# Emitting the small products of a recurrent head's scores block by block, sorted by shape

## The chip, the cores and the metric

The kernel runs on one core of a Trainium2 chip. The metric is the device time of one execution in microseconds (us); three executions of the kernel before took 1355.1, 1355.35 and 1356.38 us, median 1355.35. A profile of one execution tells when each instruction of each engine ran. TensorE multiplies matrices (PE in the profile; its weight loads are PEld), VectorE (DVE), ScalarE (ACT) and GpSimd (POOL) do the elementwise work, and SyncE (SP) issues most transfers.

## The reference

Two trunk layers over 512 latent tokens and 256 context tokens of width 1024. The first layer's mixer has eight neighbourhood attention heads and four bidirectional gated recurrent heads (HGRN2); the change lies in these four heads. Cut to that:

```python
def hgrn2_scan(q, k, v, log_f, s0):
    # S_t = diag(f_t) S_{t-1} + k_t v_t^T, o_t = S_t^T q_t, in chunks of 32 tokens
    def step(state, inp):
        qc, kc, vc, gc = inp
        bcum = jnp.cumsum(gc, axis=2)
        btot = bcum[:, :, -1:]
        qe = qc * jnp.exp(bcum)
        ke = kc * jnp.exp(-bcum)
        att = jnp.where(causal_in_chunk, jnp.einsum('bhtk,bhsk->bhts', qe, ke), 0.0)
        o = jnp.einsum('bhtk,bhkv->bhtv', qe, state) + jnp.einsum('bhts,bhsv->bhtv', att, vc)
        kd = kc * jnp.exp(btot - bcum)
        new_state = jnp.exp(btot)[:, :, 0, :, None] * state + jnp.einsum('bhsk,bhsv->bhkv', kd, vc)
        return new_state, o
...
    for d in range(2):          # forwards and backwards, each with its own gates
        ol, _ = hgrn2_scan(tr(qh), tr(k), tr(v), tr(lf), s_ctx)
        o_lat = o_lat + tr(ol)
    y = _hg_readout(o_lat, g, norm_w)
```

## The kernel before

All dense products run on TensorE in three parts (high by high, high by low, low by high part of float32; helper `mm3`, lines 246 to 248), in slices of 128 contraction rows against 512 latent or 256 context tokens. A class `Weave` puts background work between such slices: a task is a generator that yields how many slices its next step should stay behind. The order in which the code emits instructions is each engine's order, apart from what the framework's scheduler moves on the other engines; TensorE works through its list from the front, and an instruction that waits holds all behind it.

A recurrent head has two directions. `direction` makes, for each, decayed queries and keys by scans on VectorE: `qn`, `kn` within blocks of 32 tokens, `ke` for the keys of the same block, `qb` and `kb` for pairs of blocks within 128 tokens by half (GpSimd, line 608), `qi` and the states `st` at the starts of the four blocks of 128. When both directions are done, `head` runs with steps in between: `scores(0)`, `scores(1)`, `outputs(0)`, `outputs(1)`, then a root mean square.

`scores(half)` fills one bank of the accumulator memory (`pa`, 128 x 512) with four squares of 128 x 128: two blocks of 128 tokens (`nn`) by two directions (`d`). Within a square the 128-token score is put together from three kinds of products: a whole one from `ke` and `qn` (line 661), whose diagonal blocks of 32 are right; over it a 64 x 64 one from `kb` and `qb` (line 663); and over that two 32 x 32 ones from `kn` and `qn` (line 667), each with a position of its own among the array's column groups (`tile_position=(0, r0)`, r0 = 0 and 64 forwards, 32 and 96 backwards). The 64 x 64 one goes to output rows 0 to 63 forwards, 64 to 127 backwards. These are float32, which TensorE runs as two passes, so the profile counts two for each. VectorE then copies the allowed half of each square to `att` (line 671, a predicated copy) and adds the two directions to `as` (line 675); `outputs(half)` uses `as` as a weight (line 684) beside `st` and `qi` (line 682), and ScalarE starts the root mean square from the result.

Head 0's two calls have wide products between them. In heads 1, 2 and 3 the two calls come directly behind each other. The next direction's `pkc` (transposes, line 584) follows them in heads 1 and 2. Other names that the rows show: `pf`, `pfc` are the projections of gates for latent and context tokens, `pu` the state updates (line 639), `pm` an early product over four column groups (line 339), `pno` the attention's product with the values, which alternates between two 64-column tiles (line 846), `whi` and `wlo` the two parts of a weight.

Of the kernel before, what the change touches and what calls it, by code (L numbers as in the profile page):

```python
# [18 lines left out]
P = 128  # L19
# [19 lines left out]
class Weights:  # L39
    """Streams weight chunks and splits each sub-block exactly into two float32r parts."""  # L40

# [23 lines left out]
    def conv(self):  # L65
        """Split the next sub-block."""
        if self.nsub >= len(self.subs):
# [25 lines left out]
    def get(self, ahead=1):  # L93
        """The next sub-block, with some more split ahead of their use."""
        self.ahead(1 + ahead)
        r = self.ready[self.ncall]
        self.ncall += 1
        return r


class Weave:
    """Background work emitted between slices of a dense stream; a task yields the number of
    slices that its next step should stay behind."""

# [29 lines left out]
def backbone(ctx: ExitStack, tc: tile.TileContext, a, out, dump=None):  # L134
# [12 lines left out]

    # ---------------------------------------------------------------- pools
    cp = ctx.enter_context(tc.tile_pool(name="cp", bufs=1))
# [4 lines left out]

    # ---------------------------------------------------------------- weight plan
    ktiled = lambda w: w.rearrange("(k p) c -> p k c", p=P)
# [15 lines left out]
    plan = []  # L172
# [27 lines left out]

    # ---------------------------------------------------------------- constants
    cst = cp.tile([P, 769], F32, name="cst")
# [16 lines left out]

    # ================================================================ start  # L220
    m1 = ExitStack()
# [12 lines left out]
    def gate(h, src):  # L234
        """Output gate of a recurrent head with its norm weight."""
        t = zp.tile([P, T], F32, tag=f"z{4 + h}", name=f"gg{h}")
        S.activation(t[:], src, AF.Sigmoid)
        V.scalar_tensor_tensor(t[:], src, pv[:, 48 + h : 49 + h], t[:], ALU.mult, ALU.mult)
        gg[h] = t
# [10 lines left out]
    def rms(srcs, n, nm, pool, aux):  # L250
        """Reciprocal root mean square over the features."""
        acc = pool.tile([P, n], F32, tag="sqa" + nm, name="sqa" + nm, bufs=1)
# [34 lines left out]
    with ExitStack() as st:  # L287
# [36 lines left out]

        # (1 + bias) * norm weight
        wb = sp.tile([P, KT], F32, name="wb")
        V.scalar_tensor_tensor(wb[:], abT[:, 8:16], 1.0, pv[:, 16:24], ALU.add, ALU.mult)

        # adaptive shift and scale of latents and context, one feature tile at a time;
        # row blocks of the weights go to the four column groups of the array  # L330
        def normed(k):
# [29 lines left out]

        # sum of squares: odd tiles straight on the tensor engine
        acc = sp.tile([P, T], F32, name="sqax")
# [38 lines left out]

        # lower bounds of the forget gates
        lb = sp.tile([P, 24], F32, name="lb")
# [24 lines left out]
    for m in range(4):  # L429
        dbg(f"qh{m}", qf[m])  # L430
    # ---------------------------------------------------------------- remaining adaptive vectors
    class Ada:
        """Products of the remaining adaptive weights with silu(c), a row block and half a vector at a time."""

# [53 lines left out]

    # ================================================================ mixer of layer 0
    wv = Weave()  # L490
# [28 lines left out]

    # values of the recurrent heads, token-major  # L520
    wv.add(ada_units(11, 6))
# [21 lines left out]

    # ---------------------------------------------------------------- recurrent heads
    v32 = lambda t: t.rearrange("p (n t) -> p n t", t=32)
    dirs = {}

    def direction(h, d, s, sc):
# [6 lines left out]

        # weights of the context keys for the state after the context
        fc = hp.tile([P, TC + 2], F32, tag="fc", name=f"fc{nm}", bufs=1)
# [10 lines left out]

        # products of the gates within blocks of 32, up to a token and from it on
        fg = hp.tile([P, T + 2], F32, tag="fg", name=f"fg{nm}", bufs=1)  # L570
# [19 lines left out]
        V.tensor_copy(tb[:, 1:17], qn_[:, tot::32])  # L590
        # carries between blocks: [0] from the start, [1] to the end, of 128 and of 64
        cv = hp.tile([P, 4, 16], F32, tag="cv", name=f"cv{nm}", bufs=2)
# [32 lines left out]
        yield 2  # L625
        # states at the start of each block of 128
        pk = aux_t(f"pkt{nm}")
# [20 lines left out]
    def head(h):  # L648
# [5 lines left out]
        def scores(half):  # L654
            pt = aux_t(f"pa{h}{half}")
            for nn in range(2):
                n = 2 * half + nn
                for d, (qn_, kn_, ke, qi, qb, kb, st) in enumerate(hd):
                    c0 = (nn * 2 + d) * P
                    ts = slice(n * P, (n + 1) * P)  # L660
                    TE.matmul(pt[:, c0 : c0 + P], ke[:, ts], qn_[:, ts], start=True, stop=True, skip_group_check=True)
                    r0, t0 = (0, 64) if d == 0 else (64, 0)
                    TE.matmul(pt[r0 : r0 + 64, c0 + t0 : c0 + t0 + 64], kb[:, n], qb[:, n], start=True, stop=True,
                              skip_group_check=True)
                    for z in (0, 64):
                        r0, t0 = (z, z + 32) if d == 0 else (z + 32, z)
                        TE.matmul(pt[r0 : r0 + 32, c0 + t0 : c0 + t0 + 32], kn_[:, n * P + r0 : n * P + r0 + 32],
                                  qn_[:, n * P + t0 : n * P + t0 + 32], start=True, stop=True, skip_group_check=True,
                                  tile_position=(0, r0))
            a_ = att[half]  # L670
            V.copy_predicated(a_[:].rearrange("p (n c) -> p n c", n=2), dims(hgm[:], [0, 2], [1, 256]),
                              pt[:].rearrange("p (n c) -> p n c", n=2))
            am[half] = hp.tile([P, 2, P], F32, tag="as", name=f"as{h}{half}", bufs=2)
            a4 = a_[:].rearrange("p (n d c) -> p n d c", n=2, d=2)
            V.tensor_tensor(am[half][:], a4[:, :, 0], a4[:, :, 1], ALU.add)
# [16 lines left out]
        outputs(1)  # L692
        # root mean square over the head's value dimension
        sq = hp.tile([P, T], F32, tag="fg", name=f"osq{h}", bufs=1)
# [23 lines left out]

    # keys and values of the attention heads, feature-major, columns grouped by 16
    def permuted(dst, src):  # L720
# [33 lines left out]

    # ---------------------------------------------------------------- neighbourhood attention
    nas = ExitStack()
# [6 lines left out]
    def attention():  # L763
        """16 columns of queries against 32 of keys and the context at a time, two heads abreast."""
        pair, todo = {}, []
# [17 lines left out]
        def begin(p_):  # L783
            # float32r parts, stacked along the contraction: keys as (hi, lo), queries as (hi, hi) and (lo, lo)
            KS = np_.tile([P, 2, T + TC], F32R, tag="KS", name=f"KS{p_}", bufs=2)
# [122 lines left out]

    # first columns of the output projection, the last attention heads as they come
    w_first = [ws.get() for _ in range(2)]  # L910
# [11 lines left out]

    # ================================================================ the dense rest
    xp = ctx.enter_context(tc.tile_pool(name="xp", bufs=1, side="right", reuse_waits="tile"))
# [13 lines left out]
    class Norm:  # L938
        """Sum of squares over features, then the modulated norm in float32r parts."""

# [10 lines left out]
        def back(self, o, m, c, gate):  # L951
            """x += gate * o"""
            pin(V.scalar_tensor_tensor(xT[m][:, c], o[:, c], gate[:, m : m + 1], xT[m][:, c], ALU.mult, ALU.add))
# [17 lines left out]
        def outs(self, c):  # L971
            """Yields after each step of the eight feature tiles."""
            u = {}
# [12 lines left out]
    def project_back(nm, src, groups, gate, norm, start=0):  # L986
        """x += gate * (src @ w), feature-major, with the next norm; returns what the next
        phase has to emit while its first half runs."""
        A, B = HALF
# [56 lines left out]
    def pair(nm, src):  # L1046
        """Two output tiles of a 256-column chunk."""
        w = [ws.get(), ws.get()]
        o = [acc_t(f"pp{nm}{i}") for i in range(2)]
        for i in range(2):  # L1050
            mms(o[i], w[i], src, 0, 0, KT, slice(0, T), True, True)
        return o

    def quad(nm, src, rest):
        """Four output tiles, half of the tokens at a time while the norm is still on its way."""
        w = [ws.get(0) for _ in range(4)]
# [77 lines left out]

    # short convolution mixer
    mix = []
# [35 lines left out]

    # last projection, token-major
    fw = yp.tile([P, D], F32, tag="y4", name="fw")
# [107 lines left out]
```

## Time and profile before

| | kernel before |
|---|---|
| time, median of 3 runs (lowest, highest) | 1355.35 us (1355.1, 1356.38) |
| span of the profiled execution | 1353.2 us |
| median of the runs less that span | 2.15 us |
| TensorE matmuls busy | 1330.6 us, 98% |
| VectorE busy | 819.5 us, 61% |
| ScalarE busy | 527.8 us, 39% |
| GpSimd busy | 84.4 us, 6% |
| first call of `scores` starts, last ends | 131.00, 235.13 us |

The span runs from the first to the last instruction; the profiled execution has no other time of its own, so its whole time is taken as the span plus what the median of the runs lies above it. Busy time of matmuls is modelled from their starts, so a stretch in which TensorE is busy throughout can still hold time in which the array does no work; it shows in the distance from start to start.

### The profile page before, as it was taken

To read this page: it belongs to the slowest core of one execution; us is meant where nothing else is said; L and a number is where in the kernel's file an instruction comes from. 1 tells how busy PE (TensorE), PEld (TensorE's weight loads), DVE (VectorE), ACT (ScalarE), POOL (GpSimd) and SP (SyncE) were. 2 spreads that over 40 slices of the span, in tenths; PEclk is the share of its full clock that TensorE was granted. 3 is DMA by queue.
4 is the path that set the end of the run, shared out by engine and by line. 5 is a ranking of instruction groups with operands and counts; after the bars stand their busy time and mean duration, and the time that the engine had idled before them with its cause. 6 is when DMAs were issued, how large, how long until landed. Compare 5 with 4: busy or idle time off the path is not lost. (4 is left out here: it accounts for less than half of the span.)

```text
span 1353.2 us, 19127 instructions
## 1 busy us (share of the span) xinstructions
PE 1330.6 (98%) x7736; PEld 1134.4 (84%) x7736; DVE 819.5 (61%) x1354; ACT 527.8 (39%) x815; POOL 84.4 (6%) x87
## 2 busy tenths in 40 slices
PE   7999999999999999999999999999999999999997
PEld 4797888888879888888888898888998888889997
DVE  4668788687777645555566675557766544442333
ACT  4533444555555433333322253223443333333223
POOL 2204322321000000000000000000000000000000
PEclk9999999999999999999999999999999999999999
DMA  9942112466454233333366633444423222332231
GB/s 295 267 127 65 32 32 78 117 159 178 146 168 143 90 117 128 124 118 117 109 192 196 211 126 125 149 143 152 147 86 124 94 94 95 102 101 84 86 110 63
DMA packets 170824, 172.21 MB, mean 127 GB/s; under 512 B 14320, under 2 KB 144752, under 8 KB 170736
## 3 DMA queue, kind: packets, MB, share of 16 engines
q1 hardware_dynamic: 168736, 166.15, 39.3%
q10 hardware_dynamic: 2000, 4.85, 1.4%
q8 instruction: 60, 0.98, 0.3%
q14 instruction: 28, 0.23, 0.1%
HBM read 165.21 MB, written 2.10 MB: 124 GB/s over the span
## 5 line engine op out<-in xcount | busy, mean ns | idle before, releaser
L84 ACT CAST whi<-wraw 128x1024 fp32r<-128x1024 f32 (+1 forms) x202 | 207.8, 1031 | 471.1 <-PE ppv L247 93.5
L85 DVE TENSOR_TENSOR wlo<-wraw,whi 128x1024 fp32r<-128x1024 f32 (+1 forms) x202 | 242.7, 1203 | 218.9 <-ACT whi L84 217.6
L247 PE MATMUL ppa<-hf,whi 128*128 128x512 f32 (+1 forms) x448 | 161.6, 361 | 0.0
L246 PE MATMUL ppa<-hf,whi 128*128 128x512 f32 (+1 forms) x448 | 161.2, 360 | 0.0
L248 PE MATMUL ppa<-hf,wlo 128*128 128x512 f32 (+1 forms) x448 | 160.2, 358 | 0.0
L247 PE MATMUL ppv<-hf,whi 128*128 128x512 f32 x320 | 126.1, 394 | 0.0
L246 PE MATMUL ppv<-hf,whi 128*128 128x512 f32 x320 | 125.8, 393 | 0.0
L248 PE MATMUL ppv<-hf,wlo 128*128 128x512 f32 x320 | 124.3, 388 | 0.0
L462 DVE SCALAR_TENSOR_TENSOR aa<-ar,sil,aa 128x512 f32<-128x512 f32 x140 | 105.1, 751 | 15.2 <-DMA ar<-in_ada_w_dram 13.7
L1198 PE MATMUL pd<-whi,g 128*128 128x256 f32 x352 | 98.1, 279 | 0.0
L1200 PE MATMUL pd<-wlo,g 128*128 128x256 f32 x352 | 98.0, 278 | 0.0
L1199 PE MATMUL pd<-whi,g 128*128 128x256 f32 x352 | 97.7, 278 | 0.0
L246 PEld LDWEIGHTS ppa<-hf,whi 128*128 128x128 f32 x448 | 84.1, 188 | 13.9
L248 PEld LDWEIGHTS ppa<-hf,wlo 128*128 128x128 f32 x448 | 84.1, 188 | 13.2
L247 PEld LDWEIGHTS ppa<-hf,whi 128*128 128x128 f32 x448 | 84.2, 188 | 12.2
L1109 DVE TENSOR_TENSOR ppv<-ppv,cv 128x512 f32<-128x512 f32 x40 | 28.0, 699 | 86.1 <-PE ppv L248 86.1
L246 PE MATMUL pbd<-g,whi 128*128 128x512 f32 (+1 forms) x192 | 72.3, 377 | 0.0
L247 PE MATMUL pbd<-g,whi 128*128 128x512 f32 (+1 forms) x192 | 72.0, 375 | 0.0
L248 PE MATMUL pbd<-g,wlo 128*128 128x512 f32 (+1 forms) x192 | 71.7, 373 | 0.0
L246 PEld LDWEIGHTS ppv<-hf,whi 128*128 128x128 f32 x320 | 60.1, 188 | 13.8
L248 PEld LDWEIGHTS ppv<-hf,wlo 128*128 128x128 f32 x320 | 60.1, 188 | 13.4
L247 PEld LDWEIGHTS ppv<-hf,whi 128*128 128x128 f32 x320 | 60.2, 188 | 11.9
(340 smaller groups left out, 2885.3 us busy)
## 6 DMA issues: line engine op xcount, KB each, us to landing
wraw<-in_ffn_w_up_dram SPq DMA_DIRECT2D x44, 1024.0 KB, 5.0
ar<-in_ada_w_dram SPq DMA_DIRECT2D x160, 256.0 KB, 2.8
wraw<-in_ffn_w_down_dram SPq DMA_DIRECT2D x16, 1024.0 KB, 5.1
wraw<-in_od_w_in_dram SPq DMA_DIRECT2D x12, 1024.0 KB, 5.2
wraw<-in_ev_w_in_dram SPq DMA_DIRECT2D x20, 512.0 KB, 5.3
araw<-in_ada_w_dram SPq DMA_DIRECT2D x16, 512.0 KB, 6.1
wraw<-in_ffn_w_down_dram SPq DMA_DIRECT2D x8, 768.0 KB, 4.9
wraw<-in_ev_w_out_dram SPq DMA_DIRECT2D x4, 1024.0 KB, 6.8
```

The costliest lines, as they stand in the source:

```text
L84: self.nc.scalar.copy(hv, rv)
L85: self.pin(self.nc.vector.tensor_tensor(lv, rv, hv.bitcast(F32), ALU.subtract))
L246: TE.matmul(o, wh, mh, start=start, stop=False, skip_group_check=True)
L247: TE.matmul(o, wh, ml, start=False, stop=False, skip_group_check=True)
L248: TE.matmul(o, wl, mh, start=False, stop=stop, skip_group_check=True)
L462: pin(V.scalar_tensor_tensor(self.acc[:], raw[:], sil[:, r, 0:1], self.acc[:], ALU.mult, ALU.add))
L1109: V.tensor_tensor(ov[i][:], ov[i][:], t[i][:], ALU.mult)
L1198: TE.matmul(o[i][:, 0:256], gh[:, ts], w[0][:, k - k0], start=k == 0, stop=False)
L1199: TE.matmul(o[i][:, 0:256], gl[:, ts], w[0][:, k - k0], start=False, stop=False)
L1200: TE.matmul(o[i][:, 0:256], gh[:, ts], w[1][:, k - k0], start=False, stop=k == FT - 1)
```

## The change

In `scores` the loops are turned round: first the four 128-column products of the call, then its four 64 x 64 ones, then its eight 32 x 32 ones, directions alternating within each block. Products, operands, targets and their number stay. Comments and docstrings are taken out too, with the line numbers kept up to line 655; behind the changed lines all numbers are 7 higher (line 663 becomes 667, 667 becomes 674, 671 becomes 678, 675 becomes 682, 682 becomes 689, 684 becomes 691).

```diff
         def scores(half):
             pt = aux_t(f"pa{h}{half}")
+            col = lambda nn, d: (nn * 2 + d) * P
+            both = [(nn, d) for nn in range(2) for d in range(2)]
+            for nn, d in both:
+                qn_, kn_, ke, qi, qb, kb, st = hd[d]
+                ts = slice((2 * half + nn) * P, (2 * half + nn + 1) * P)
+                TE.matmul(pt[:, col(nn, d) : col(nn, d) + P], ke[:, ts], qn_[:, ts], start=True, stop=True,
+                          skip_group_check=True)
+            for nn, d in both:
+                qn_, kn_, ke, qi, qb, kb, st = hd[d]
+                r0, t0 = (0, 64) if d == 0 else (64, 0)
+                c0 = col(nn, d) + t0
+                TE.matmul(pt[r0 : r0 + 64, c0 : c0 + 64], kb[:, 2 * half + nn], qb[:, 2 * half + nn], start=True,
+                          stop=True, skip_group_check=True)
             for nn in range(2):
-                n = 2 * half + nn
-                for d, (qn_, kn_, ke, qi, qb, kb, st) in enumerate(hd):
-                    c0 = (nn * 2 + d) * P
-                    ts = slice(n * P, (n + 1) * P)
-                    TE.matmul(pt[:, c0 : c0 + P], ke[:, ts], qn_[:, ts], start=True, stop=True, skip_group_check=True)
-                    r0, t0 = (0, 64) if d == 0 else (64, 0)
-                    TE.matmul(pt[r0 : r0 + 64, c0 + t0 : c0 + t0 + 64], kb[:, n], qb[:, n], start=True, stop=True,
-                              skip_group_check=True)
-                    for z in (0, 64):
-                        r0, t0 = (z, z + 32) if d == 0 else (z + 32, z)
-                        TE.matmul(pt[r0 : r0 + 32, c0 + t0 : c0 + t0 + 32], kn_[:, n * P + r0 : n * P + r0 + 32],
-                                  qn_[:, n * P + t0 : n * P + t0 + 32], start=True, stop=True, skip_group_check=True,
-                                  tile_position=(0, r0))
+                for z, d in [(z, d) for z in (0, 64) for d in range(2)]:
+                    qn_, kn_, ke, qi, qb, kb, st = hd[d]
+                    r0, t0 = (z, z + 32) if d == 0 else (z + 32, z)
+                    c0, n0 = col(nn, d) + t0, (2 * half + nn) * P
+                    TE.matmul(pt[r0 : r0 + 32, c0 : c0 + 32], kn_[:, n0 + r0 : n0 + r0 + 32],
+                              qn_[:, n0 + t0 : n0 + t0 + 32], start=True, stop=True, skip_group_check=True,
+                              tile_position=(0, r0))
```

On TensorE the first call of head 0 stood like this before (`pa00` is the bank of head 0's first half; `00` and `01` in `qn00`, `ke01` are head and direction):

```order
L661 MATMUL pa00_1364<-qn00_1116,ke00_1164 128x128
L663 MATMUL pa00_1364<-qb00_1191,kb00_1189 64x64
L667 MATMUL pa00_1364<-qn00_1116,kn00_1117 32x32 x2
L661 MATMUL pa00_1364<-qn01_1233,ke01_1281 128x128
L663 MATMUL pa00_1364<-qb01_1308,kb01_1306 64x64
L667 MATMUL pa00_1364<-qn01_1233,kn01_1234 32x32 x2
```

These six rows come a second time for the next 128 tokens, so the shape of the products changes three times in each group of four products.

The same call in the changed kernel, on TensorE, with the wide product that follows it (the first half of each block for one 128-token stretch, the second for the next):

```order
L661 MATMUL pa00_1364<-qn00_1116,ke00_1164 128x128
L661 MATMUL pa00_1364<-qn01_1233,ke01_1281 128x128
...
L667 MATMUL pa00_1364<-qb00_1191,kb00_1189 64x64
L667 MATMUL pa00_1364<-qb01_1308,kb01_1306 64x64
...
L674 MATMUL pa00_1364<-qn00_1116,kn00_1117 32x32
L674 MATMUL pa00_1364<-qn01_1233,kn01_1234 32x32
...
L246 MATMUL pf11_1333<-h0_3_88,whi7_1209 128x512
```

Four, four and eight products of a shape now stand together. The rows ahead of the call and behind it are the same as before.

In head 1 the two calls meet on TensorE. Before, the end of the first (`pa10`) and the start of the second (`pa11`) were:

```order
L663 MATMUL pa10_1662<-qb11_1606,kb11_1604 64x64
L667 MATMUL pa10_1662<-qn11_1531,kn11_1532 32x32 x2
L661 MATMUL pa11_1688<-qn10_1353,ke10_1448 128x128
L663 MATMUL pa11_1688<-qb10_1483,kb10_1481 64x64
L667 MATMUL pa11_1688<-qn10_1353,kn10_1354 32x32 x2
```

In the changed kernel the same place on TensorE, from the first 64 x 64 product of direction 1 on, which waits for GpSimd's `qb11`:

```order
L667 MATMUL pa10_1662<-qb11_1606,kb11_1604 64x64
...
L674 MATMUL pa10_1662<-qn11_1531,kn11_1532 32x32
L661 MATMUL pa11_1688<-qn10_1353,ke10_1448 128x128
L661 MATMUL pa11_1688<-qn11_1531,ke11_1579 128x128
...
L584 MATMUL pkc20_1714<-cst_70,sc20_1622 128x128 x2
```

What waits for `qb11` has moved behind all four 128-column products of its call; `pkc20` still follows the two calls. The orders of VectorE, ScalarE, GpSimd and the transfer queues are those of the kernel before, row for row.

## Rows read from the trace of the kernel before

**Rows 1.** The page: engines' busy time, share and instructions; then the costliest group.
```profile
PE 1330.6 (98%) x7736; PEld 1134.4 (84%) x7736; DVE 819.5 (61%) x1354; ACT 527.8 (39%) x815; POOL 84.4 (6%) x87
...
L84 ACT CAST whi<-wraw 128x1024 fp32r<-128x1024 f32 (+1 forms) x202 | 207.8, 1031 | 471.1 <-PE ppv L247 93.5
```

**Rows 2.** Windows: stretch, length, each engine's busy time, granted clock, DMA share, GB/s.
```profile
18.00:20.00 2.00, 2.00 (x9) 1.14 (x11) 1.05 (x2) 0.83 (x1) 0.07 (x1) 0.54 1.18 318
...
165.00:172.00 7.00, 6.63 (x63) 4.76 (x62) 5.12 (x8) 0.00 (x0) 3.46 (x4) 1.00 0.00 0
```

**Rows 3.** Timeline, TensorE, head 0's first call: start, length, instruction, count [idle before].
```profile
131.00 0.38 PE L661 MATMUL pa<-qn,ke 128*128 128x128 f32 x2
131.31 0.33 PE L663 MATMUL pa<-qb,kb 128*64 128x64 f32 x2
131.57 0.26 PE L667 MATMUL pa<-qn,kn 128*32 128x32 f32 x4
131.75 0.49 PE L661 MATMUL pa<-qn,ke 128*128 128x128 f32 x2
132.17 0.33 PE L663 MATMUL pa<-qb,kb 128*64 128x64 f32 x2
...
134.34 0.50 PE L246 MATMUL pf<-h,whi 128*128 128x512 f32 x1
```

**Rows 4.** Timeline, TensorE: four full-array passes on end in head 0's outputs.
```profile
144.10 0.60 PE L682 MATMUL po<-qi,st 128*128 128x128 f32 x4
```

**Rows 5.** Timeline, TensorE, windows so narrow that later passes stand alone.
```profile
131.97 0.28 PE L661 MATMUL pa<-qn,ke 128*128 128x128 f32 x1
...
131.42 0.22 PE L663 MATMUL pa<-qb,kb 128*64 128x64 f32 x1
...
131.62 0.20 PE L667 MATMUL pa<-qn,kn 128*32 128x32 f32 x2
```

**Rows 6.** Timeline, TensorE: products on two and on four column tiles.
```profile
272.72 1.09 PE L846 MATMUL pno<-pT,vn 128*64 128x128 f32 x16
273.75 0.51 PE L248 MATMUL pv<-h,wlo 128*128 128x512 f32 x1
...
19.83 1.07 PE L339 MATMUL pm<-araw,sil 128*32 128x256 f32 x16
20.84 0.50 PE L247 MATMUL pq<-h,w0h 128*128 128x512 f32 x1
```

**Rows 7.** Timeline, GpSimd: `qb` of direction 1 in heads 1 and 3.
```profile
165.70 0.80 POOL L608 TENSOR_TENSOR qb<-qn,cv 128x256 f32<-128x256 f32 x1
...
228.58 0.61 POOL L608 TENSOR_TENSOR qb<-qn,cv 128x256 f32<-128x256 f32 x1
```

**Rows 8.** Timeline, TensorE: head 1's calls and what follows; head 3's start.
```profile
164.93 0.39 PE L661 MATMUL pa<-qn,ke 128*128 128x128 f32 x2
...
166.55 0.33 PE L663 MATMUL pa<-qb,kb 128*64 128x64 f32 x2 [0.37 <-POOL qb L608]
...
172.17 0.44 PE L584 MATMUL pkc<-cst,sc 128*128 128x128 f32 x2
...
173.92 0.38 PE L684 MATMUL po<-as,vh 128*128 128x128 f32 x2
...
228.34 0.39 PE L661 MATMUL pa<-qn,ke 128*128 128x128 f32 x2
```

**Rows 9.** Timeline, VectorE: `as` in head 0, then head 1 and its `qh`.
```profile
136.63 0.41 DVE L675 TENSOR_TENSOR as<-att 128x256 f32<-128x256 f32 x1
...
169.42 0.69 DVE L671 COPY_PREDICATED att<-hgm,pa 128x512 f32<-128x512 int32 x1
172.28 0.74 DVE L671 COPY_PREDICATED att<-hgm,pa 128x512 f32<-128x512 int32 x1 [2.17 <-PE pa L667]
172.92 0.74 DVE L675 TENSOR_TENSOR as<-att 128x256 f32<-128x256 f32 x2
...
184.18 0.69 DVE L701 TENSOR_TENSOR qh<-po,osq 128x512 f32<-128x512 f32 x1 [1.39 <-ACT osq L700]
```

## The prediction

> **What bounds the kernel now.** I read the page's first part first: TensorE's matmuls are busy 98% of the span and no other engine comes near [rows 1]. The clock that the throttle granted is full where the changed code runs [rows 2]. So a microsecond taken out of TensorE's own row of work is a microsecond off the end, unless TensorE then has to wait. The second view is the timeline of TensorE over one call of `scores` (half a head), which shows what the row of small products is made of. The third is the timeline of the engines that feed it (GpSimd's `qb`) and of the one that takes its result (VectorE's `att` and `as`), because these decide what is late once the products are quicker.
>
> In the timeline each float32 product counts twice (x2 for one product): the engine runs it as two passes, each with its own weight load. So a call has 8 passes of 128 columns, 8 of 64 and 16 of 32. The first call runs from 131.00 to 134.34, 3.34 us [rows 3], in four equal cells of 128, 64, 32. The reader is to see that a cell's length isn't the work in it. Full-array float32 passes that follow each other start 0.11 us apart: a row of four lasts 0.60, its last one 0.28, which leaves 0.32 for three steps [rows 4, 5]. The pair at 131.00, entered from a wide product of the same shape, takes 0.31 to the next shape, and the pair at 131.75, entered from the 32-column products, 0.42 [rows 3]. So 0.11 is a weight load that could not be done beforehand, and the last pass of a shape costs 0.20 to the next shape's start (131.97 to 132.17) where 0.11 is its work: about 0.09 to 0.10 us in which the array empties. The 64-column pair has the same: 0.11 from first to second pass, of which half is a load in the open, then 0.15 from 131.42 to 131.57. The 32-column passes: 0.05 to the second round at 131.62, then 0.13 [rows 3, 5]. Each change of shape therefore costs an emptying of about 0.10 plus one exposed load (0.11, 0.055 or 0.027 by width), and a call has three per cell, twelve in all.
>
> **The change, part by part.** It emits the same 16 products in three blocks, so a call has three changes of shape instead of twelve. Nothing else moves: the other engines' orders are as before, and on TensorE only the rows within a call are rearranged.
>
> *128-column block.* Eight passes: seven steps of 0.11 and a last one of 0.20, 0.97 us (0.11 more where the call is entered from 32-column products).
>
> *64-column block.* Before never runs more than two passes on end there, so the inner step is unknown. Bounds: 0.056 (half the full-array step, for half the columns) and 0.107 (a load in the open each time). The products alternate between the two halves of the array's columns. How such tiles run is shown at L846: 16 passes of 128 moving columns, alternating between two 64-column tiles, take 1.03 us up to the next shape [rows 6], eight rounds of 0.11 and the tail; singly they would need 16 steps of 0.11, 1.8 us. So two tiles run side by side. Here that makes four rounds: 0.11 + 2 x 0.056 + a stagger of 0.01 + 0.15 = 0.38 us. One after the other it would be 0.11 + 6 x 0.056 + 0.15 = 0.60.
>
> *32-column block.* Sixteen passes in four column groups, in the group order 0, 32, 64, 96. L339 does the same with 256 moving columns: 16 passes in 1.01 us [rows 6], where one such pass is some 0.21 (twice 0.107), so four abreast in four rounds. Here: 0.05 + 2 x 0.03 + stagger 0.02 + 0.13 = 0.26 us; one after the other 0.05 + 14 x 0.028 + 0.13 = 0.57. I take the side-by-side value for both blocks, by the rows of the same form.
>
> Sum of a call: 0.97 + 0.38 + 0.26 = 1.61 against 3.34, so 1.73 saved; eight calls, 13.8 us.
>
> A rule of the Trainium skill speaks against the short last block: the page "TensorE: Matmul & The Clock Gate" (section "Wait — 56ns, not 53.3ns?") says that matmuls never start less than about 25 ns apart, however small. The trace disagrees for neighbouring column tiles: both passes that start at 131.62 stand in one row of 0.20, the length of a single one [rows 5]. By the rule the 32-column block would be 16 x 0.025 + 0.13 = 0.53, a call would save 1.46, and the time, by the sums below (2.9 for heads 0 and 3, 2.72 for 1 and 2), would be 1344.1; its chance is counted with rival A's.
>
> *What is late next.* In heads 1 and 2 both calls stand together, 164.93 to 172.17, and hold a wait of TensorE for GpSimd: direction 1's `qb` ends at 166.50 [rows 7] and its first 64-column product starts at 166.55 [rows 8]. That product now comes 0.97 us behind the call's start instead of 1.17 (0.31 + 0.26 + 0.18 + 0.42), so from about 165.9 to 166.55 TensorE has one 64-column product of direction 0 to do and stands for the rest; everything behind is held (half 0's remaining small products, all of half 1, then `pkc`). From 166.55: 0.37 (0.11 + 2 x 0.056 + 0.15) + 0.26 + the second call 1.72 (with its 0.11 more) brings `pkc` to 168.90 instead of 172.17, 3.27 saved. Then TensorE meets L684, which reads `as`, 1.75 behind `pkc` (173.92 - 172.17), now at 170.65. VectorE makes `as` in its own order: the first `att` copy at 169.42 with no idle time before it, so it can't come sooner; the second follows 0.64 later (the step 172.28 to 172.92), now without its 2.17 of idle; the first `as` starts at 170.70 and takes 0.41 [rows 9]. TensorE gets on at 171.17 (170.70 + 0.41, and some 0.05 for the signal, as from `qb`'s end to the product behind it), not 170.65. The saving of heads 1 and 2 is 173.92 - 171.17 = 2.75 each. In head 3 `qb` is done at 229.19 [rows 7] and wanted at 228.34 + 0.97 = 229.31 [rows 8], just in time, and no `pkc` hurries behind the calls; in head 0 the calls stand apart with wide products between. These two keep 2 x 1.73 = 3.46 each.
>
> Sum: 3.46 + 2.75 + 2.75 + 3.46 = 12.4 us. Behind the heads I take nothing back: ScalarE's weight conversions sit idle before them, mostly for TensorE [rows 1], and move up with it. The span of 1353.2 falls to 1340.8; the runs' median stands 2.15 above that span, so I add this and get **1343.0**.
>
> **Rivals.**
> *A. The small passes don't run abreast* (each fed singly, or the engine can't be fed so fast). Speaking for it: before never has more than four such short passes on end. Against: L339 and L846. A call is then 0.97 + 0.60 + 0.57 = 2.14 and saves 1.20; heads 0 and 3 give 2.40 each, heads 1 and 2 about 2.31 (the wait for `as` is gone then): 9.4 us, 1346.0.
> *B. VectorE becomes the bound of heads 1 and 2.* It is idle 2.17 and 1.39 us in such a head (before the second `att` and before `qh`) [rows 9]. If only the first can be had, these heads give 2.17 each: 11.3 us, 1344.1. For it: the gap-free row of VectorE up to 169.42. Against: the idle time before `qh` is a wait on a chain that starts from TensorE's own outputs and moves up with them.
> *C. It doesn't do what it says:* a change of column tile stops the array as a change of shape does. Then the 64-column block is 4 x 0.26 and the 32-column one 8 x 0.18, a call 3.45, and with the earlier wait on `qb` the time is about 1356, no change. Against it is L846 with its rounds of 0.11 for two tiles. The Trainium skill's page "TensorEngine Tiling (Array Packing)" (section "Key Properties") says that a change of tiling mode drains the engine and a change of tile doesn't; the trace agrees (the same rounds of 0.11).
> *D. Slower: the clock.* The granted clock fell to 0.54 at 18 to 20 us, early in the kernel, and is 1.00 through the calls [rows 2]. If the denser blocks of narrow products, with the longer stand at `qb`, made it fall to 1.2 GHz behind each head, every microsecond of full-speed work would take two; the gain of 3.1 per head is eaten from 3.1 us of such work on. At 4 us per head it is 16 - 12.4 = 3.6 slower, 1359. For it: TensorE idles more in one piece. Against: the piece is some 0.6 us, while the clock stayed full across 165 to 172, where a stand of 0.37 lies.
>
> **How the numbers follow.** Forecast 66% (its own range 1341.5 to 1345), A 14%, B 12%, C 5%, D 3%. A measurement of this kernel can tell about 0.2%, 2.7 us. The forecast, A and B are all faster by more: 92%. C is the same: 5%. D: 3% slower. The range runs from 1340.5 (no wait for `as`, and shorter tails than I took) to 1348 (A with a wait more).
>
> **What would show it.** In the changed profile a call of head 0 should last about 1.6 us, with the four 128-column products in 0.97 and the 32-column ones in 0.26 (0.57 would be A; 1.4 would be C). Behind the calls of heads 1 and 2 the idle time before the second `att` should be gone, and TensorE should wait some 0.5 us for `as` and some 0.6 for `qb`. From head 0's first call to 245 us the stretch should be 12.4 us shorter, and the rest as long as before. I am wrong if the calls shrink and the span doesn't: then a wait that I did not name has taken it.

## The result, and the profile after

The changed kernel takes 1343.47 us (median of 4 runs, 1342.99 to 1344.03) against 1355.37 (4 runs of the kernel before); the ratio is 0.991, 95% interval 0.9896 to 0.9924. That is 11.9 us faster; 1343.0 was forecast. Seven further runs were made as experiments, six of other kernels and one of the changed kernel again.

The page of the changed kernel, span and engines, against [rows 1]:

```profile
span 1341.5 us, 19127 instructions
...
PE 1318.2 (98%) x7736; PEld 1126.1 (84%) x7736; DVE 821.3 (61%) x1354; ACT 527.9 (39%) x815; POOL 84.4 (6%) x87
```

The same instructions ran, and TensorE lost 12.4 us of busy time while its share stayed 98%: the bound is where it was and its row of work is shorter.

Timeline of TensorE, changed kernel: head 0's first call (start, length, instruction, count), against [rows 3]; then the start of head 3 and the first product behind its last call:

```profile
131.51 1.05 PE L661 MATMUL pa<-qn,ke 128*128 128x128 f32 x8
132.50 0.45 PE L667 MATMUL pa<-qb,kb 128*64 128x64 f32 x8
132.88 0.33 PE L674 MATMUL pa<-qn,kn 128*32 128x32 f32 x16
133.14 0.50 PE L246 MATMUL pf<-h,whi 128*128 128x512 f32 x1
...
220.00 1.06 PE L661 MATMUL pa<-qn,ke 128*128 128x128 f32 x8
...
223.36 0.71 PE L689 MATMUL po<-qi,st 128*128 128x128 f32 x4
```

Three rows stand where there were twelve. From start to start the blocks take 0.99, 0.38 and 0.26 us, the call 1.63 instead of 3.34. From the first call's start to the last one's end it is 223.36 - 131.51 = 91.85 us, before 235.13 - 131.00 = 104.13: 12.28 less. What follows is 1118.1 us long in both (1341.46 - 223.36 and 1353.18 - 235.13). The 0.5 us that is missing in the span (11.72 less) went ahead of the first call, where the changed code plays no part.

Timeline of TensorE, changed kernel, both calls of head 1 and what follows, against [rows 8]:

```profile
162.01 1.06 PE L661 MATMUL pa<-qn,ke 128*128 128x128 f32 x8
163.00 0.33 PE L667 MATMUL pa<-qb,kb 128*64 128x64 f32 x2
163.63 0.45 PE L667 MATMUL pa<-qb,kb 128*64 128x64 f32 x6 [0.30 <-POOL qb L608]
164.00 0.33 PE L674 MATMUL pa<-qn,kn 128*32 128x32 f32 x16
164.26 1.16 PE L661 MATMUL pa<-qn,ke 128*128 128x128 f32 x8
...
166.00 0.44 PE L584 MATMUL pkc<-cst,sc 128*128 128x128 f32 x2
...
168.18 0.49 PE L691 MATMUL po<-as,vh 128*128 128x128 f32 x2 [0.27 <-DVE as L682]
```

GpSimd's `qb` and VectorE in the same stretch and at `qh`, changed kernel, against [rows 7, 9]:

```profile
162.78 0.80 POOL L608 TENSOR_TENSOR qb<-qn,cv 128x256 f32<-128x256 f32 x1
```

```profile
164.82 1.76 DVE L577 TENSOR_TENSOR_SCAN kn<-fg,cst 128x512 f32<-128x512 f32 x1
166.50 1.32 DVE L678 COPY_PREDICATED att<-hgm,pa 128x512 f32<-128x512 int32 x2
167.71 0.74 DVE L682 TENSOR_TENSOR as<-att 128x256 f32<-128x256 f32 x2
...
178.55 0.69 DVE L708 TENSOR_TENSOR qh<-po,osq 128x512 f32<-128x512 f32 x1 [1.05 <-ACT osq L707]
```

Two things are to be seen. The six passes at 163.63 start 0.05 behind the end of `qb` (163.58): TensorE has come to that wait earlier. In head 0 the first passes of the two directions start together (the 64-column block alternates between them); here direction 1's starts 0.63 behind direction 0's, where 0.6 was forecast. The idle times in brackets are shorter than these stands, since they count from the modelled ends of the passes ahead. And VectorE's two `att` copies now stand in one row: the 2.17 us of idle time between them [rows 9] is gone. In its place the new wait stands, L691 for `as`: 168.18 is 0.06 behind the end of the first `as` (167.71 + 0.41).

The granted clock from the first call to 245 us, behind all four heads (windows: stretch, length, busy time by engine, clock, DMA share, GB/s), against [rows 2]:

```profile
131.00:245.00 114.00, 112.36 (x855) 96.93 (x855) 94.50 (x156) 58.05 (x90) 35.21 (x37) 1.00 0.23 59
```

### The profile page after: what moved, and what is told of

The parts are those of the page before. It is cut to its first block, busy times and chain, and to the rows that moved or that the text cites. A ratio compares the mean times of both kernels' runs of the same rounds, so it can differ in the third digit from the quotient of the medians.

```text
span 1341.5 us, 19127 instructions
## 1 busy us (share of the span) xinstructions
PE 1318.2 (98%) x7736; PEld 1126.1 (84%) x7736; DVE 821.3 (61%) x1354; ACT 527.9 (39%) x815; POOL 84.4 (6%) x87
## 5 line engine op out<-in xcount | busy, mean ns | idle before, releaser
L247 PEld LDWEIGHTS ppv<-hf,whi 128*128 128x128 f32 x320 | 60.2, 188 | 11.9
```

Source lines behind the costliest of these rows:

```text
L247: TE.matmul(o, wh, ml, start=False, stop=False, skip_group_check=True)
```

## The experiments

The theory is the prediction's: each change of shape empties the array and leaves a weight load in the open, and short products on different column tiles run side by side. Rival 1 gives the gain to the running side by side alone; rival 2 holds that the stand at `qb` decides in heads 1 and 2 (these two are the experiments' own and not the prediction's A to D). The measure that is least disturbed is the stretch from the first call's start to the last call's end in each profile; before 104.13, changed 91.85. Ratios are against runs of the kernel before on the same chip (median 1356.07 us for the kernels with nine changes, sixteen changes, same-tile neighbours and `qb` last; 1355.48 for the other three).

**Nine changes of shape instead of three.** The diffs stand against the changed kernel; where they have `whole`, `mid` and `small`, its three products are put into functions of these names. The 32-column products of a square, emitted after all 64-column ones in the change, stand behind its 64-column one.

```diff
-            for nn, d in both:
-                mid(nn, d)
...
+            for nn, d in both:
+                mid(nn, d)
+                small(nn, d, 0)
+                small(nn, d, 64)
```

> The four 128-column products of a call stand together, the 64- and 32-column ones alternate as before: nine changes of shape per call instead of twelve. Theory (each change of shape empties the array and leaves a weight load in the open): a call of head 0 takes 0.97 + 4 x (0.26 + 0.18) = 2.73 us, heads 0 and 3 save 1.2 us each, heads 1 and 2 some 1.45 each: 5.3 us, about 1350. Rival 1 (the gain comes from short products on different column tiles running side by side, a change of shape by itself costs little): only the hidden loads of the 128-column products are won, 3 x 0.11 per call, a call of 3.0 us, about 1352.7.

Measured 1350.9 us, ratio 0.996 (0.9945 to 0.9975). TensorE, head 0's first call, and the end of head 3's:

```profile
132.39 1.05 PE L662 MATMUL pa<-qn,ke 128*128 128x128 f32 x8
133.38 0.33 PE L669 MATMUL pa<-qb,kb 128*64 128x64 f32 x2
133.63 0.26 PE L676 MATMUL pa<-qn,kn 128*32 128x32 f32 x4
133.82 0.33 PE L669 MATMUL pa<-qb,kb 128*64 128x64 f32 x2
...
135.15 0.50 PE L246 MATMUL pf<-h,whi 128*128 128x512 f32 x1
...
231.32 0.71 PE L698 MATMUL po<-qi,st 128*128 128x128 f32 x4
```

A pair of 64 and its four passes of 32 take 0.44 again and again, as in the kernel before. The call is 2.76 us (2.73 expected, rival 1 said 3.0), the stretch 98.93, 5.2 us less than before (5.3 expected). So rival 1 falls as the sole cause.

**Sixteen changes of shape.**

```diff
             for nn, d in both:
                 whole(nn, d)
+                small(nn, d, 0)
                 mid(nn, d)
-                small(nn, d, 0)
                 small(nn, d, 64)
```

> Within each square the order is 128, 32, 64, 32: sixteen changes of shape per call. Theory: a square takes 0.42 + 0.18 + 0.26 + 0.18 = 1.04, a call of head 0 4.05 us instead of 3.34; heads 0 and 3 lose 1.4 each, heads 1 and 2 about 1.06 each (their stand at qb shrinks): 5 us slower than the kernel before, about 1360. Rival 1: the two 32-column products of a square, no longer side by side, cost 0.03 to 0.05 more per square, 0.2 per call, about 1357.

Measured 1360.84 us, ratio 1.0041 (1.0023 to 1.006): slower than before. TensorE, the first square of the first call, the call's end, and head 3's end:

```profile
132.83 0.38 PE L662 MATMUL pa<-qn,ke 128*128 128x128 f32 x2
133.15 0.25 PE L676 MATMUL pa<-qn,kn 128*32 128x32 f32 x2
133.32 0.33 PE L669 MATMUL pa<-qb,kb 128*64 128x64 f32 x2
133.58 0.25 PE L676 MATMUL pa<-qn,kn 128*32 128x32 f32 x2
133.76 0.49 PE L662 MATMUL pa<-qn,ke 128*128 128x128 f32 x2
...
136.86 0.50 PE L246 MATMUL pf<-h,whi 128*128 128x512 f32 x1
...
241.78 0.71 PE L697 MATMUL po<-qi,st 128*128 128x128 f32 x4
```

One 32-column product alone between two other shapes takes 0.17 to 0.18 us, as long as two of them take side by side in the kernel before (131.57 to 131.75, [rows 3]). Of that some 0.06 is its two passes, by the 0.03 us a pass of the one-tile kernel below; the larger part goes with the change. The call is 4.03 us (4.05 expected), the stretch 108.95, 4.8 longer (5 expected). This profile's last projection was also 4 us longer than in the other profiles; that lies far behind the heads, and why is open.

**Three changes, products on the same tile next to each other.**

```diff
-            for nn, d in both:
-                mid(nn, d)
-            for nn in range(2):
-                for z, d in [(z, d) for z in (0, 64) for d in range(2)]:
-                    small(nn, d, z)
+            for d in range(2):
+                for nn in range(2):
+                    mid(nn, d)
+            for d in range(2):
+                for z in (0, 64):
+                    for nn in range(2):
+                        small(nn, d, z)
```

> Three blocks by shape as in the change, but products on the same column tile stand next to each other (64-column ones: forwards twice, then backwards twice; 32-column ones: both of a group, then the next group). Three changes of shape per call, as in the change. If only neighbours on different tiles run side by side: 64-column block 0.60, 32-column block 0.57, a call 2.14 us, about 1346. If the engine finds work for another tile at any distance in its queue: a call 1.6 us as in the change, about 1343.5. Rival 1 expects the first, and more: most of the gain of the change gone.

Measured 1344.07 us, ratio 0.9906 (0.9891 to 0.9921). TensorE, first call of head 0, then head 1's 64-column products from the one that waits for `qb`:

```profile
132.28 1.05 PE L662 MATMUL pa<-qn,ke 128*128 128x128 f32 x8
133.26 0.46 PE L669 MATMUL pa<-qb,kb 128*64 128x64 f32 x8
133.65 0.35 PE L676 MATMUL pa<-qn,kn 128*32 128x32 f32 x16
133.93 0.50 PE L246 MATMUL pf<-h,whi 128*128 128x512 f32 x1
...
164.45 0.45 PE L669 MATMUL pa<-qb,kb 128*64 128x64 f32 x4 [0.19 <-POOL qb L608]
```

Blocks of 0.39 and 0.28, a call of 1.65, the stretch 91.89: as in the change. In head 1 four passes now wait for `qb`, where six did in the change: direction 0's four stand ahead of them, so the products are on TensorE in the order written. Standing next to each other is not needed; the first case of the expectation is out. The run does not yet show that running side by side is worth anything, since it left that in place.

**The same with a single tile, so that nothing can run side by side.**

```diff
-                TE.matmul(pt[r0 : r0 + 64, c0 : c0 + 64], ...)
+                TE.matmul(pt[0:64, c0 : c0 + 64], ...)
...
-                    TE.matmul(pt[r0 : r0 + 32, c0 : c0 + 32], ..., tile_position=(0, r0))
+                    TE.matmul(pt[0:32, c0 : c0 + 32], ..., tile_position=(0, 0))
```

Its scores land in the wrong rows, so this kernel serves for its time alone.

> The change with all 64-column products written by the first column tile and all 32-column ones by the first column group, so that none can run side by side; the 128-column products read kn in place of ke, to keep the values finite. The result is not the reference's. Three changes of shape per call. Theory (changes of shape, and beside them short products side by side): 64-column block 0.60 us instead of 0.38, 32-column block 0.57 instead of 0.26, a call 2.14 us; about 1346 (as comes a little later in VectorE's order here, up to 1 us more). If only the number of changes counts: a call 1.6 us, 1343.5. Rival 1 (side by side is most of the gain): a call of 2.9 us or more, over 1350.

Measured 1347.26 us, ratio 0.9937 (0.9924 to 0.9951). TensorE, head 0's first call and head 3's end:

```profile
131.57 1.05 PE L661 MATMUL pa<-qn,kn 128*128 128x128 f32 x8
132.55 0.68 PE L667 MATMUL pa<-qb,kb 128*64 128x64 f32 x8
133.16 0.69 PE L674 MATMUL pa<-qn,kn 128*32 128x32 f32 x16
133.78 0.50 PE L246 MATMUL pf<-h,whi 128*128 128x512 f32 x1
...
227.57 0.71 PE L689 MATMUL po<-qi,st 128*128 128x128 f32 x4
```

Blocks of 0.61 and 0.62 instead of 0.38 and 0.26: a call of 2.21, 0.58 longer than in the change at the same number of changes of shape. The stretch is 96.00. So of the 1.71 us that a call of head 0 saves, 1.13 are there without any side by side (3.34 to 2.21) and 0.58 come with it; both rivals that knew only one of them are out. The division is not a sharp one: the kernel before already runs its two 32-column products of a square side by side (both in 0.18), and the one-tile kernel gives that up. By its 0.03 us a pass that is some 0.06 for each of four squares, so as an estimate fewer changes are worth 1.13 to 1.36 and side by side 0.35 to 0.58. Twelve changes on a single tile were not run. The framework's scheduler moved a few products of TensorE and `as` in this kernel, so its time is rougher than its call. (It does move TensorE's products too, which the text on the kernel before leaves to the other engines.)

**The products that wait for `qb` last.**

```diff
             for nn, d in both:
                 whole(nn, d)
-            for nn, d in both:
-                mid(nn, d)
...
+            for nn, d in both:
+                mid(nn, d)
```

> Blocks in the order 128, 32, 64, so that the products that wait for qb come last in their call. Theory: a call of head 0 as long as in the change (1.6 us); in heads 1 and 2 TensorE stands some 0.25 us less at qb, pkc comes about 0.26 earlier, but the first product with as starts where it starts in the change, because VectorE sets it: the time is that of the change, 1343.5, within 0.3. Rival 2 (the stand at qb decides in heads 1 and 2): the product with as starts 0.26 earlier in both heads too, 0.5 us off the time.

Measured 1343.68 us, ratio 0.9912 (0.9895 to 0.9928). TensorE, head 1:

```profile
162.03 1.06 PE L662 MATMUL pa<-qn,ke 128*128 128x128 f32 x8
...
165.76 0.44 PE L584 MATMUL pkc<-cst,sc 128*128 128x128 f32 x2
...
168.21 0.49 PE L702 MATMUL po<-as,vh 128*128 128x128 f32 x2 [0.53 <-DVE as L693]
```

`pkc` comes 3.73 us after the head's start instead of 3.99, and the product with `as` 6.18 after it, in the change 6.17. What was saved at `qb` is waited for `as`: 0.53 instead of 0.27. The stretch is 91.85, the very one of the change.

**Both halves as one call.** The new function emits 8 whole, 8 64-column and 16 32-column products of both halves, then `att` and `as` of both.

```diff
-        scores(0)
-        yield 2
-        scores(1)
-        yield 2
+        both_scores()
+        yield 4
         outputs(0)
```

> Both calls of a head as one: eight 128-column products, then eight 64-, then sixteen 32-column ones, three changes of shape per head instead of six; then both halves of att and as. Theory: the calls of a head take 1.88 + 0.61 + 0.37 = 2.86 us instead of 3.26 (head 0) and 3.36 (head 3); in heads 1 and 2 the stand at qb is gone (the first 64-column product is due 1.88 us after the start, qb is there at 1.62) and pkc comes 1.1 us earlier, but VectorE still sets the first product with as, so nothing more is won there: 0.9 us less than the change, about 1342.6, less than the times can tell. Rival 2 (the stand at qb decides in heads 1 and 2): 0.8 more in each, about 1341.

Measured 1344.1 us, ratio 0.9913 (0.99 to 0.9927). TensorE in head 1, with the first product of head 0 that reads `as` ahead of it; then VectorE in both heads:

```profile
139.29 0.49 PE L695 MATMUL po<-as,vh 128*128 128x128 f32 x2 [1.12 <-DVE as L686]
...
162.97 1.95 PE L661 MATMUL pa<-qn,ke 128*128 128x128 f32 x16
164.85 0.69 PE L667 MATMUL pa<-qb,kb 128*64 128x64 f32 x16
165.46 0.46 PE L674 MATMUL pa<-qn,kn 128*32 128x32 f32 x32
165.85 0.44 PE L584 MATMUL pkc<-cst,sc 128*128 128x128 f32 x2
...
169.12 0.49 PE L695 MATMUL po<-as,vh 128*128 128x128 f32 x2 [1.10 <-DVE as L686]
```

```profile
136.94 0.75 DVE L613 SCALAR_TENSOR_TENSOR kn<-kn,oml,s 128x512 f32<-128x512 f32 x1
137.60 1.33 DVE L682 COPY_PREDICATED att<-hgm,pa 128x512 f32<-128x512 int32 x2
...
167.46 1.30 DVE L682 COPY_PREDICATED att<-hgm,pa 128x512 f32<-128x512 int32 x2
168.66 0.74 DVE L686 TENSOR_TENSOR as<-att 128x256 f32<-128x256 f32 x2
```

The calls take 2.88 us (2.86 expected) and there is no stand at `qb`, yet the product with `as` comes 6.15 us after the head's start, as ever. Rival 2 is out by both runs. The expected 0.9 us were not won: in head 0 the emission of both copies behind both calls put them behind `kn` on VectorE, and TensorE waits 1.1 us for `as` there too. From head 0's first call to head 1's it is 31.38 us (162.97 - 131.59), in the change 30.50 (162.01 - 131.51); the stretch is 92.22.

**The change once more.**

> The changed kernel once more, as the measure for the two others on the same chip: 1343.5 us, within 0.2%, by every theory.

Measured 1343.83 us, ratio 0.9911 (0.9897 to 0.9924), the stretch 91.84. The versions with three changes of shape and tiles side by side can't be told apart by their times; none beats the change.

## Why the prediction was right

*A call.* Forecast 0.97 + 0.38 + 0.26 = 1.61, measured 0.99 + 0.38 + 0.26 = 1.63. Head 0 gained 3.34 + 3.34 - 1.63 - 1.63 = 3.42 (3.46 forecast). The two blocks that the kernel before did not show were taken from lines of the same form (L846, L339), and the one-tile run gives the other end of the bounds: 0.61 and 0.62 against 0.60 and 0.57.

*What is late next.* The stand at `qb` and the wait for `as` came where they were put. L691 is at 168.18, where 166.00 + 1.75 = 167.75 would be due: 0.43 late, 0.52 forecast. Heads 1 and 2 gave 2.71 each (2.75 forecast): from head 1's first call to head 3's it was 63.41 us (164.93 to 228.34, [rows 8]) and is 57.99 (162.01 to 220.00). Head 3 needed no wait: its calls take 3.36 (220.00 to 223.36) where they took 6.79, 3.43 less (3.46).

*The sum.* 12.4 was forecast for the heads, 12.28 came (3.43 from head 0's first call to head 1's, 5.42, 3.43). That the gain goes through to the end undiminished was the least worked-out step; the rest of the kernel is 1118.1 us long before and after, so it held. That the medians came within 0.5 us of the forecast is in part luck: the first call's start alone shifts by more than that from one profile to the next (last section). Of the 2.15 us set on top of the span some 0.3 are such a difference between executions too: in the later runs each time lies 1.74 to 1.86 us above its own span.

*The rivals.* A (no side by side) asked for a call of 2.14; the one-tile kernel is that case, with calls of 2.21, and cost 3.4 us over the change in the times (1347.26 against 1343.83, both on the same chip), 4.15 in the stretch. B asked for idle time before `qh` that stays; it shrank from 1.39 to 1.05, and the heads gave more than 2.17. What B says of VectorE is right as far as the forecast had it: its order of work sets the first product with `as`. C is refuted by the blocks of 0.38 and 0.26. D: the clock is 1.00 through the calls and behind them, 131 to 245 us.

*The rule of 25 ns* (the Trainium skill, "TensorE: Matmul & The Clock Gate", section "Wait — 56ns, not 53.3ns?") would have made the last block 0.53 us long, by the prediction's estimate. In the change sixteen passes and their tail take 0.26, so it does not bind across column tiles. On a single tile the sixteen passes need 0.62; less the tail of 0.13 that is 0.03 us for each, above the rule's floor.

*What a change costs.* TensorE and its weight loads in head 0's first call of the changed kernel, the last 128-column pass and the first loads of the next shape:

```profile
132.29 0.28 PE L661 MATMUL pa<-qn,ke 128*128 128x128 f32 x1
...
132.49 0.31 PEld L667 LDWEIGHTS pa<-qb,kb 128*64 128x64 f32 x8
```

The next shape's first load stands 0.20 us behind the start of the last pass. Within a shape on one tile the next pass starts after 0.11 (128 columns), 0.06 (64) or 0.03 (32): the one-tile blocks, less their tail and their first step, give (0.61 - 0.15 - 0.11) / 6 and (0.62 - 0.13 - 0.05) / 14. Across a change it is 0.20, 0.15 and 0.13 [rows 3, 5], so each shape that is left costs about the same, 0.09 to 0.10 more. A rival not named so far is that a product must wait for the write that it overwrites: before, a 64-column product goes over a corner of the square just written (131.97 to 132.17). In the change the last 128-column pass and the first 64-column one belong to different squares, and the distance is the same (132.29 to 132.50), so that is not the cause.

What stays argued and not shown: that the 0.10 us at each change is the array emptying. The records show that no pass and no load starts in it, and not what the array does.

## What to carry to other kernels

Where a busy TensorE runs short products, read the distance from start to start at each change of tile shape, not the busy share: here a change in front of a 128-column product cost 0.19 us (0.58 for three), nearly as much as the product's two passes (2 x 0.11). Sorting the products by shape took half of the time of a call without removing one, a part of it because products of a shape on different column tiles could then run side by side. Count the changes, and look for a line elsewhere in the same trace that already runs the sorted form, for its price. Then follow the consumers: once the products are quicker, another engine's order of work (here VectorE's `as`) sets the next start, and filling the wait ahead of it wins nothing.

## What was not expected of the hardware

TensorE does not need neighbours to run tiles side by side: with four passes on each column group in a row, the 32-column block still took 0.28 us against 0.62 on one group, and the 64-column block 0.39 against 0.61. Had the passes started in the order of their emission, the fifth could not have come before the four on its neighbour tile, and the expectation's 0.60 and 0.57 would have shown. So a pass on a free tile starts ahead of earlier ones that queue for another tile, and the text on the kernel before, by which TensorE works through its list from the front, is too simple there. For a wait it holds: in head 1 of the changed kernel a direction 0 product stands behind the first that waits for `qb`, on the free tile, and starts only with it (x2 at 163.00, x6 at 163.63).

The start of the kernel varies more than the change's finest terms: the first call starts between 131.00 and 132.83 us in the nine profiles, although nothing ahead of it differs, while the stretch of the heads repeats to 0.01 us (91.85 and 91.84).
